# Second feed-forward of a two-layer backbone: products of 512 columns for the high weight halves, and feature sums spread out

## The chip, the cores and the metric

The kernel runs on one core of one Trainium2 chip, as one program and one launch. The metric is device time in microseconds. The kernel before took 2392.74 us, the median of 3 runs (2392.0 to 2393.63). One execution was also recorded by the hardware profiler, and every row quoted below is from that record.

The engines in the profile are PE (TensorE, the matmuls; PEld are its weight loads), DVE (VectorE), ACT (ScalarE), POOL (GpSimd) and SP, whose queue issues the transfers from memory.

## The reference, cut to what matters

Two trunk layers run over two groups of 128 tokens each (a prompt and a latent sample) with the same weights. Each layer is a mixer followed by a gated convolutional feed-forward, with an adaptive norm (shift, scale and gate computed from a condition vector) around both. The feed-forward is the part that the change touches:

```python
def conv_ffn(h, w_up, w_conv, b_conv, w_down):
    u = h @ w_up
    up = jnp.pad(u, ((0, 0), (1, 1), (0, 0)))
    u = up[:, :-2] * w_conv[0] + up[:, 1:-1] * w_conv[1] + up[:, 2:] * w_conv[2] + b_conv
    gate, val = u[..., :D_FF], u[..., D_FF:]
    return (jax.nn.silu(gate) * val) @ w_down

mod = jax.nn.silu(cond) @ w_ada[l] + b_ada[l]
sh1, sc1, gt1, sh2, sc2, gt2 = jnp.split(mod[:, None, :], 6, axis=-1)
x = x + gt2 * conv_ffn(h, w_ffn_up[l], w_ffn_conv[l], b_ffn_conv[l], w_ffn_down[l])
```

The model width is 2048, D_FF is 5632, and everything is float32.

## The kernel before

**Layout.** All activations lie with features on the 128 partitions and tokens along the free dimension. The two groups stand side by side, so an operand has NT = 256 columns.

**Split products.** A float32 product is made of three float32r products. Every operand x is kept as a high half (x rounded to float32r) and a low half (the rest), next to each other: `hx[:, k, :256]` and `hx[:, k, 256:512]`, and likewise the feed-forward's inner tiles `g`. Every 128 x 128 weight block is split in the same way into `wh` and `wl`, when it has been loaded: ACT casts the high half (L204), DVE subtracts to get the low half (L205), 8 blocks at a time. `gemm` (L278) then runs over the blocks of a product and issues wh x high (L285), wh x low (L286) and wl x high (L287), all three into the same 256 columns of a PSUM bank `acc`. There are three such banks, four buffers each for `wh` and `wl`, and three for the loaded tiles `raw` of 16 blocks.

**The feed-forward.** `ffn` (L919) runs in two rounds, each over half of the inner features. `up` (L941) makes 44 products of 16 blocks, alternately gate and value. After each, `conv` (L928) reads the bank three times: ACT (L930) and twice DVE (L933, L936). A pair is then multiplied and split into a `g` tile. `down` (L959) makes 16 products of 22 blocks over these g tiles, and `residual` (L512) adds each to x by two DVE operations (L515). In the last round the squares of x are summed on the way, for the final norm. The first three of the 88 up products of a layer are made by `first_three` (L255) while the norm before them is still running; they come to `ffn` in the list `ready`.

**Work in between.** The shifts, scales and gates come from a product with `w_ada`, 201 MB of weights for two columns. They are cut into units (layer, part, quarter) and made beside the rest of the kernel in two ways. Some units run on PE (`row_step`). Others are feature sums on DVE (`feature_step`, L355, recorded on L363): one pass of DVE over a 128 x 2048 tile for each of the two conditions, so that a loaded tile `araw` serves two sums and a unit takes eight. `pump` (L428) is called after each product and counts a rate up; when a whole step is due it issues one. In the up-projections the rate of feature sums is `FRATE["up"]`, 0.75 for each product. In the second feed-forward three units are left for the feature sums: 24 sums, the gate of its own residual. So after the first `up`, `ensure(l, 5)` issues all that are still missing, before the first `down`.

**Order.** The program is written in the order of the code. A scheduler then orders each engine's instructions by a simulated timeline, and on the chip each engine takes them strictly in that order. The feature sums keep the order of the code among themselves. Transfers are issued by SP in order, and each waits there until its buffer is free.

Of the kernel before, what the change touches and what calls it, by code (L numbers as in the profile page):

```python
# [13 lines left out]
ALU = mybir.AluOpType  # L14
# [3 lines left out]
P = 128  # L18
# [3 lines left out]
NT = 2 * T  # L22
# [26 lines left out]
    _n += _w  # L49
NCONST = _n  # L50
RATE = {"in": 0.4, "in3": 0.25, "heads": 0.85, "out0": 1.2, "c": 0.65, "outc": 0.65}
FRATE = {"up": 0.75, "down": 1.47}
PEW = {"heads": 1.0, "out0": 1.0, "c": 0.5}
QUIET = [4, 3, 3]

# [4 lines left out]
LATE = 3  # L60
# [21 lines left out]
def step_kernel(ctx: ExitStack, tc: tile.TileContext, A: dict):  # L82
    nc = tc.nc
    pe, dve, act, pool, sp = nc.tensor, nc.vector, nc.scalar, nc.gpsimd, nc.sync
# [3 lines left out]
    tmp = ctx.enter_context(tc.tile_pool(name="tmp", bufs=2))  # L88
    small = ctx.enter_context(tc.tile_pool(name="small", bufs=4))
    pacc = ctx.enter_context(tc.tile_pool(name="pacc", bufs=3, space=PSUM))  # L90
# [5 lines left out]
    def banks(name):  # L96
        return tc.tile_pool(name=name, bufs=1, space=PSUM)
# [3 lines left out]
    def nm(s):  # L101
        uid[0] += 1
        return f"{s}_{uid[0]}"

    def T_(pl, shape, tag, dt=F32, bufs=None):
        kw = {} if bufs is None else {"bufs": bufs}
        return pl.tile(shape, dt, tag=tag, name=nm(tag), **kw)
# [95 lines left out]
    def split(out_hi, out_lo, src):  # L203
        act.copy(out_hi, src)  # L204
        dve.tensor_tensor(out=out_lo, in0=src, in1=out_hi.bitcast(F32), op=ALU.subtract)  # L205
# [72 lines left out]
    def gemm(blocks, xh, xl, n=NT, first=0):  # L278

        ps = T_(pacc, [P, 512], "acc")  # L280
        last = len(blocks) - 1
        for i in range(last + 1):
            k = (i + first) % (last + 1)
            wh, wl = blocks[k]
            pe.matmul(ps[:, :n], wh, xh(k), start=(i == 0), stop=False)  # L285
            pe.matmul(ps[:, :n], wh, xl(k), start=False, stop=False)  # L286
            pe.matmul(ps[:, :n], wl, xh(k), start=False, stop=(i == last))  # L287
        return ps[:, :n]

# [57 lines left out]
    def load_row():  # L349
        feat["row"] = T_(feat["home"], [P, 2, D], "condb")  # L350
        sp.dma_start(out=feat["row"], in_=A["condb"])
        for r in range(2):
            act.activation(feat["row"][:, r], feat["row"][:, r], AF.Silu)

    def feature_step():  # L355

        l, j, q = FEATS[feat["i"]]
        t, c = divmod(feat["t"], 2)
        out = mod[:, l, j, 4 * q:4 * q + 4]
        if c == 0:  # L360
            feat["raw"] = T_(wpool, [P, 4, 512], "araw", bufs=2)
            sp.dma_start(out=feat["raw"], in_=A["w_ada"][l, j, q, t])
        tc.keep_in_program_order(dve.tensor_tensor_reduce(  # L363
            out=T_(feat["pool"], [P, D], "junk"), in1=feat["row"][:, c],
            in0=feat["raw"].rearrange("p g n -> p (g n)"), scale=1.0, scalar=0.0,
            op0=ALU.mult, op1=ALU.add, accum_out=out[:, t, c:c + 1]))
        feat["t"] += 1
        if feat["t"] == 8:
            dve.tensor_tensor(out=out, in0=out, in1=vector("bada", l, j, q), op=ALU.add)
            scales(l, j, q, out)  # L370
            feat["i"] += 1
            feat["t"] = 0
# [55 lines left out]
    def pump(rows, feats=0.0, until=None):  # L428

        until = until or RLIMIT[stage[0]]  # L430
        step()
        ada["due"] += rows
        while ada["due"] >= 0.25:
            if ada["i"] >= until and not later:
                ada["due"] = 0.0
                break
            dve_or_none = ada["i"] >= until or ada["i"] in SUMMED
            ada["due"] -= 0.25 if dve_or_none else 0.25 * ada["pew"]
            row_step(until)
        feat["due"] += feats  # L440
        while feat["due"] >= 1.0 and feat["i"] < FLIMIT[stage[0]]:
            feat["due"] -= 1.0
            feature_step()

    def ensure(l, j, qs=range(4)):
        for u in [(l, j, q) for q in qs]:
            while u in ROWS and ada["i"] <= ROWS.index(u):
                row_step()
            while u in FEATS and u not in done:
                feature_step()  # L450
            while u not in done:
                later.pop(0)()
# [59 lines left out]
    def residual(ps, l, which, c, st=None):  # L512
        for g in range(2):
            s = slice(g * T, (g + 1) * T)
            dve.scalar_tensor_tensor(out=x[:, c, s], in0=ps[:, s],  # L515
                                     scalar=mod[:, l, 3 * which + 2, c, g:g + 1],
                                     in1=x[:, c, s], op0=ALU.mult, op1=ALU.add)
        if st is not None:
            stat_add(st, x[:, c], KD)
# [398 lines left out]

    def ffn(hx, W, ready, l, st):  # L919
        xh, xl = (lambda k: hx[:, k, :NT]), (lambda k: hx[:, k, NT:2 * NT])  # L920
        product = lambda: ready.pop(0) if ready else gemm(W.chunk(), xh, xl)
        WD = Weights(A["w_down"][l], KQ, TB)
        cw = ada["cw"]
        with tc.tile_pool(name=f"ffn{l}", bufs=1) as fp, banks(f"pffn{l}") as pf:
            feat["home"], feat["pool"] = fp, pf
            T_(fp, [P, SHIFT // 4], "pad")

            def conv(ps, m):  # L928
                y = T_(fp, [P, NT], "cv", bufs=3)
                act.activation(y, ps, AF.Identity, scale=cw[:, 1, m:m + 1], bias=cw[:, 3, m:m + 1])  # L930
                y3 = y.rearrange("p (g t) -> p g t", g=2)
                p3 = ps.rearrange("p (g t) -> p g t", g=2)
                dve.scalar_tensor_tensor(out=y3[:, :, 1:], in0=p3[:, :, :T - 1],  # L933
                                         scalar=cw[:, 0, m:m + 1], in1=y3[:, :, 1:],
                                         op0=ALU.mult, op1=ALU.add)
                dve.scalar_tensor_tensor(out=y3[:, :, :T - 1], in0=p3[:, :, 1:],  # L936
                                         scalar=cw[:, 2, m:m + 1], in1=y3[:, :, :T - 1],
                                         op0=ALU.mult, op1=ALU.add)
                return y

            def up(q):  # L941
                gs = []
                for i in range(q * KQ, (q + 1) * KQ):
                    rate = 0 if i < LATE else FRATE["up"]
                    fine[0] = False
                    gate = conv(product(), i)
                    pump(0, rate)
                    if i == 0:
                        load_row()
                    val = conv(product(), NFF + i)  # L950
                    pump(0, rate)
                    act.activation(gate, gate, AF.Silu)
                    dve.tensor_tensor(out=val, in0=gate, in1=val, op=ALU.mult)
                    g = T_(fp, [P, ROW], "g", F32R, bufs=KQ)
                    split(g[:, :NT], g[:, NT:2 * NT], val)
                    gs.append(g)
                return gs

            def down(gs, q):  # L959
                for c in range(KD):  # L960
                    quiet = q == NQ - 1 and c >= KD - QUIET[0]
                    fine[0] = quiet
                    ps = gemm(WD.chunk(), lambda k: gs[k][:, :NT], lambda k: gs[k][:, NT:2 * NT])
                    residual(ps, l, 1, c, st if q == NQ - 1 else None)
                    pump(0, 0 if quiet else FRATE["down"])

            for q in range(NQ):
                gs = up(q)
                if q == 0:
                    ensure(l, 5)  # L970
                down(gs, q)
            while feat["i"] < FLIMIT[stage[0]]:
                feature_step()


    with banks("pab") as ppool["ada"]:
# [8 lines left out]
        hx = T_(keep, [P, KD, ROW], "hx", F32R)  # L985
# [3 lines left out]
        W = Weights(A["w_up"][0], KD, 1)  # L989
        hx, ready = modulated(st, 0, 1, W)  # L990
    stage[0] = "ffn0"
    st = stat_init()
    ffn(hx, W, ready, 0, st)
    stage[0] = "c"
    with tc.tile_pool(name="cc", bufs=1) as cp, banks("pc") as ppool["ada"]:
        ada["pool"] = cp
        ppool["att"] = ppool["ada"]
        W = Weights(A["w_in_c"], KD, 1)
        hx, ready = modulated(st, 1, 0, W)
# [4 lines left out]
        W = Weights(A["w_up"][1], KD, 1)  # L1004
        hx, ready = modulated(st, 1, 1, W)
    stage[0] = "ffn1"
    st = stat_init()
    ffn(hx, W, ready, 1, st)
    rb = norm_scale(st)
    for c in range(KD):  # L1010
# [131 lines left out]
```

## Time and profile before

| | |
|---|---|
| Median of 3 runs | 2392.74 us |
| The profiled execution | 2393.78 us |
| Its span, first to last instruction | 2391.9 us |
| Mean granted TensorE clock | 0.986 |
| Mean transfer rate from memory | 256 GB/s |
| First feed-forward, about | 505 to 1200 us |
| Second feed-forward, about | 1660 to 2377 us |
| Its first and second down-projection begin at | 1898.2 and 2257.2 us |

A row of the page's groups names the line, the engine, the operation, the tiles (written <- read), the shape and the count; then the busy time and the mean duration in ns, and the idle time of the engine ahead of these instructions with what ended it. Matmuls are pipelined: the recorded time of one runs into the next, and the distance between the starts of two tells what one costs. In the chain of waits each row is a start, a length and a piece of work, back from the last instruction.

### The profile page before, as it was taken

To read this page: it belongs to the slowest core of one execution; us is meant where nothing else is said; L and a number is where in the kernel's file an instruction comes from. 1 tells how busy PE (TensorE), PEld (TensorE's weight loads), DVE (VectorE), ACT (ScalarE), POOL (GpSimd) and SP (SyncE) were. 2 spreads that over 40 slices of the span, in tenths; PEclk is the share of its full clock that TensorE was granted. 3 is DMA by queue.
4 is the path that set the end of the run, shared out by engine and by line. 5 is a ranking of instruction groups with operands and counts; after the bars stand their busy time and mean duration, and the time that the engine had idled before them with its cause. 6 is when DMAs were issued, how large, how long until landed. Compare 5 with 4: busy or idle time off the path is not lost.

```text
span 2391.9 us, 47258 instructions
## 1 busy us (share of the span) xinstructions
PE 2321.7 (97%) x19628; PEld 2189.1 (92%) x19628; DVE 1782.0 (75%) x2714; ACT 1161.1 (49%) x1814; POOL 176.0 (7%) x211
## 2 busy tenths in 40 slices
PE   6999999999999999999989999998999999999997
PEld 3778868789999999999979999997999999999997
DVE  2457544479999999999977798886899755666654
ACT  4435545355554345554454454445555534555542
POOL 2002101110000000001210000122000000000011
PEclk8999999999999999999989999999999999999999
DMA  9886677877777877777857777776677555555553
GB/s 377 319 334 243 231 272 305 314 288 256 270 266 283 299 277 265 267 265 284 302 225 275 268 270 292 249 272 252 224 265 265 195 194 194 194 194 194 194 194 122
DMA packets 92551, 612.93 MB, mean 256 GB/s; under 512 B 9969, under 2 KB 17841, under 8 KB 20401
## 3 DMA queue, kind: packets, MB, share of 16 engines
q1 hardware_dynamic: 92336, 609.91, 69.5%
q8 instruction: 154, 2.52, 0.4%
q14 instruction: 61, 0.49, 0.1%
HBM read 605.12 MB, written 4.75 MB: 255 GB/s over the span
## 4 chain that ended last, share of the span: by engine, by line
PE 92%; DVE 3%; DMA 3%; issue 1%; ACT 1%; POOL 0%; SPq 0%; POOLq 0%; DVEq 0%; ACTq 0%
PE acc L285 27%; PE acc L286 27%; PE acc L287 27%; PE ada L378 4%; DMA araw<-w_ada 1%; PE acc L269 1%; DVE aacc L407 1%; PE acc L270 1%; DVE wl L205 1%; PE acc L271 1%; PE att L564 1%; DMA ckc<-cache_ckv 1%; DMA raw<-w_in_ab 0%; PE ada L326 0%; PE att L855 0%
## 5 line engine op out<-in xcount | busy, mean ns | idle before, releaser
L204 ACT CAST wh<-raw 128x1024 fp32r<-128x1024 f32 (+1 forms) x788 | 793.9, 1013 | 984.4 <-PE acc L286 868.8
L205 DVE TENSOR_TENSOR wl<-raw,wh 128x1024 fp32r<-128x1024 f32 (+1 forms) x788 | 923.5, 1184 | 388.6 <-ACT wh L204 383.9
L285 PE MATMUL acc<-hx,wh 128*128 128x256 f32 x4064 | 1132.3, 279 | 9.2 <-ACT hx L472 6.2
L286 PE MATMUL acc<-hx,wh 128*128 128x256 f32 x4064 | 1130.2, 278 | 0.0
L287 PE MATMUL acc<-hx,wl 128*128 128x256 f32 x4064 | 1129.9, 278 | 0.0
L285 PEld LDWEIGHTS acc<-hx,wh 128*128 128x128 f32 x4064 | 765.7, 189 | 36.6 <-issue 13.0
L286 PEld LDWEIGHTS acc<-hx,wh 128*128 128x128 f32 x4064 | 766.1, 189 | 15.3 <-issue 14.4
L287 PEld LDWEIGHTS acc<-hx,wl 128*128 128x128 f32 x4064 | 765.6, 188 | 9.3 <-issue 9.1
L286 PE MATMUL acc<-g,wh 128*128 128x256 f32 x1408 | 388.2, 276 | 0.0
L287 PE MATMUL acc<-g,wl 128*128 128x256 f32 x1408 | 388.1, 276 | 0.0
L285 PE MATMUL acc<-g,wh 128*128 128x256 f32 x1408 | 388.0, 276 | 0.0
L363 DVE CUSTOM_DVE_ANT_0 junk<-araw,condb 128x2048 f32<-128x2048 f32 x128 | 293.2, 2291 | 0.0
L286 PEld LDWEIGHTS acc<-g,wh 128*128 128x128 f32 x1408 | 264.2, 188 | 0.0
L287 PEld LDWEIGHTS acc<-g,wl 128*128 128x128 f32 x1408 | 264.2, 188 | 0.0
L285 PEld LDWEIGHTS acc<-g,wh 128*128 128x128 f32 x1408 | 264.1, 188 | 0.0
L170 POOL TENSOR_TENSOR sqacc<-sqacc,sq 128x256 f32<-128x256 f32 x76 | 93.8, 1234 | 1529.2 <-issue 1223.1
L378 PE MATMUL ada<-araw,condw 128*32 128x512 f32 x832 | 116.6, 637 | 27.7 <-DMA araw<-w_ada 22.7
L407 DVE SCALAR_TENSOR_TENSOR aacc<-araw,condw,aacc 128x512 f32<-128x512 f32 x150 | 112.4, 773 | 0.2
L930 ACT ACTIVATE cv<-acc,convw 128x256 f32<-128x256 f32 x176 | 98.1, 559 | 0.0
L515 DVE SCALAR_TENSOR_TENSOR x<-acc,mod,x 128x128 f32<-128x128 f32 x192 | 58.4, 344 | 45.3 <-PE acc L287 44.3
L936 DVE SCALAR_TENSOR_TENSOR cv<-acc,convw,cv 128x254 f32<-128x254 f32 x176 | 84.4, 480 | 3.8
L933 DVE SCALAR_TENSOR_TENSOR cv<-acc,convw,cv 128x254 f32<-128x254 f32 x176 | 83.7, 476 | 0.0
(207 smaller groups left out, 1812.9 us busy)
## 6 DMA issues: line engine op xcount, KB each, us to landing
araw<-w_ada SPq DMA_DIRECT2D x188, 1024.0 KB, 5.6
raw<-w_up SPq DMA_DIRECT2D x176, 1024.0 KB, 4.8
raw<-w_down SPq DMA_DIRECT2D x88, 1024.0 KB, 4.8
raw<-w_in_c SPq DMA_DIRECT2D x48, 1024.0 KB, 5.5
raw<-w_in_ab SPq DMA_DIRECT2D x20, 1024.0 KB, 7.2
raw<-w_out_ab SPq DMA_DIRECT2D x16, 1024.0 KB, 6.9
raw<-w_out_c SPq DMA_DIRECT2D x16, 1024.0 KB, 4.8
raw<-w_q_up SPq DMA_DIRECT2D x6, 768.0 KB, 4.7
```

The costliest lines, as they stand in the source:

```text
L170: pool.tensor_tensor(out=st["acc"], in0=st["acc"], in1=sq, op=ALU.add)
L204: act.copy(out_hi, src)
L205: dve.tensor_tensor(out=out_lo, in0=src, in1=out_hi.bitcast(F32), op=ALU.subtract)
L285: pe.matmul(ps[:, :n], wh, xh(k), start=(i == 0), stop=False)
L286: pe.matmul(ps[:, :n], wh, xl(k), start=False, stop=False)
L287: pe.matmul(ps[:, :n], wl, xh(k), start=False, stop=(i == last))
L363: tc.keep_in_program_order(dve.tensor_tensor_reduce(out=T_(feat["pool"], [P, D], "junk"), in1=feat["row"][:, c], in0=feat["raw"].rearrange ...
L378: i = pe.matmul(ada["ps"][32 * g:32 * g + 32, :], condw[:, 4 * t + g, :], raw[:, g], start=(t == 0), stop=(t == 3), skip_group_check=True)
L407: i = dve.scalar_tensor_tensor(out=acc[:, c], in0=raw[:, g], scalar=condw[:, k, c:c + 1], in1=acc[:, c], op0=ALU.mult, op1=ALU.add)
L930: act.activation(y, ps, AF.Identity, scale=cw[:, 1, m:m + 1], bias=cw[:, 3, m:m + 1])
L933: dve.scalar_tensor_tensor(out=y3[:, :, 1:], in0=p3[:, :, :T - 1], scalar=cw[:, 0, m:m + 1], in1=y3[:, :, 1:], op0=ALU.mult, op1=ALU.add)
L936: dve.scalar_tensor_tensor(out=y3[:, :, :T - 1], in0=p3[:, :, 1:], scalar=cw[:, 2, m:m + 1], in1=y3[:, :, :T - 1], op0=ALU.mult, op1=ALU.add)
```

## The change

In the second feed-forward (layer index 1) `gemm` is replaced by `gemm_wide`. The high weights meet both halves of the operand in one matmul of 512 columns, which writes the whole bank: wh x high into the first 256 columns, wh x low into the others. The matmul of the low weights adds wl x high to the second 256. In the last block the low weights come first. The two halves of the bank are summed on the way out: ACT copies the second half to a tile `nt`, DVE adds the first half to it, and `conv` and `residual` read this tile in place of the bank. The three products of `first_three` stay as they were, and so does the first feed-forward.

The rate of the feature sums in the up-projection becomes one for each layer: 0.75 in the first, as before, and 0.35 in the second.

```diff
-FRATE = {"up": 0.75, "down": 1.47}
+FRATE = {"up": (0.75, 0.35), "down": 1.47}
...
+    def gemm_wide(blocks, x2):
+        ps = T_(pacc, [P, 512], "acc")
+        last = len(blocks) - 1
+        for i, (wh, wl) in enumerate(blocks):
+            if i < last:
+                pe.matmul(ps, wh, x2(i), start=(i == 0), stop=False)
+            pe.matmul(ps[:, NT:], wl, x2(i)[:, :NT], start=False, stop=False)
+        pe.matmul(ps, wh, x2(last), start=False, stop=True)
+        u = T_(tmp, [P, NT], "nt", bufs=4)
+        act.copy(u, ps[:, NT:])
+        dve.tensor_tensor(out=u, in0=ps[:, :NT], in1=u, op=ALU.add)
+        return u
...
-        product = lambda: ready.pop(0) if ready else gemm(W.chunk(), xh, xl)
+        wide = l == 1
+
+        def product():
+            if ready:
+                return ready.pop(0)
+            return gemm_wide(W.chunk(), lambda k: hx[:, k]) if wide else gemm(W.chunk(), xh, xl)
...
-                    rate = 0 if i < LATE else FRATE["up"]
+                    rate = 0 if i < LATE else FRATE["up"][l]
...
-                    ps = gemm(WD.chunk(), lambda k: gs[k][:, :NT], lambda k: gs[k][:, NT:2 * NT])
+                    if wide:
+                        ps = gemm_wide(WD.chunk(), lambda k: gs[k])
+                    else:
+                        ps = gemm(WD.chunk(), lambda k: gs[k][:, :NT], lambda k: gs[k][:, NT:2 * NT])
```

The built programs show what this moves. In the rows below a number behind a name tells one buffer from the next.

PE, the first two blocks of the first down-projection's first product, before:

```order
L285 MATMUL acc_22356<-g_19566,wh_22338 128x256
L286 MATMUL acc_22356<-g_19566,wh_22338 128x256
L287 MATMUL acc_22356<-g_19566,wl_22339 128x256
L285 MATMUL acc_22356<-g_19638,wh_22338 128x256
L286 MATMUL acc_22356<-g_19638,wh_22338 128x256
L287 MATMUL acc_22356<-g_19638,wl_22339 128x256
```

and the first three blocks of it now:

```order
L297 MATMUL acc_21823<-g_19566,wh_21805 128x512
L298 MATMUL acc_21823<-g_19566,wl_21806 128x256
L297 MATMUL acc_21823<-g_19625,wh_21805 128x512
L298 MATMUL acc_21823<-g_19625,wl_21806 128x256
L297 MATMUL acc_21823<-g_19730,wh_21805 128x512
L298 MATMUL acc_21823<-g_19730,wl_21806 128x256
```

A block is two matmuls where it was three; each has one weight load of its own.

DVE, where the first down-projection begins (`g` is the last g tile's low half, `wl` are low halves of weights, `junk` are feature sums), before:

```order
L205 TENSOR_TENSOR g_22333<-cv_22327,g_22333 128x256
L205 TENSOR_TENSOR wl_22432<-raw_22425,wh_22431 128x1024
L515 SCALAR_TENSOR_TENSOR x_76<-acc_22356,mod_77,x_76 128x128 x2
L205 TENSOR_TENSOR wl_22507<-raw_22504,wh_22506 128x1024
L205 TENSOR_TENSOR wl_22511<-raw_22504,wh_22510 128x1024
L205 TENSOR_TENSOR wl_22517<-raw_22514,wh_22516 128x1024
L515 SCALAR_TENSOR_TENSOR x_76<-acc_22435,mod_77,x_76 128x128 x2
```

and now:

```order
L205 TENSOR_TENSOR g_21766<-cv_21760,g_21766 128x256
L378 ISA junk_21769,mod_77<-araw_21655,condb_19556 128x2048
L378 ISA mod_77 128x1
L378 ISA junk_21773,mod_77<-araw_21771,condb_19556 128x2048
L378 ISA mod_77 128x1
L205 TENSOR_TENSOR wl_21936<-raw_21933,wh_21935 128x1024
L302 TENSOR_TENSOR nt_21868<-acc_21823,nt_21868 128x256
L378 ISA junk_21775,mod_77<-araw_21771,condb_19556 128x2048
L378 ISA mod_77 128x1
L205 TENSOR_TENSOR wl_21940<-raw_21933,wh_21939 128x1024
L530 SCALAR_TENSOR_TENSOR x_76<-nt_21868,mod_77,x_76 128x128 x2
L205 TENSOR_TENSOR wl_21946<-raw_21943,wh_21945 128x1024
```

All 24 feature sums of this stage stood ahead of this place before. Now 13 do, and 11 stand behind it, among the first eight down products. The sum of the bank's two halves (L302) stands ahead of each residual (L530).

PE, where that first down product (acc_22356 before, acc_21823 now) reads the last g tile in its last block, before:

```order
L285 MATMUL acc_22356<-g_22333,wh_22348 128x256
L285 MATMUL acc_22435<-g_19566,wh_22348 128x256
L286 MATMUL acc_22435<-g_19566,wh_22348 128x256
L287 MATMUL acc_22435<-g_19566,wl_22349 128x256
L285 MATMUL acc_22435<-g_19638,wh_22348 128x256
L286 MATMUL acc_22356<-g_22333,wh_22348 128x256
L287 MATMUL acc_22356<-g_22333,wl_22349 128x256
```

and now, behind seventeen matmuls of the next product, acc_21883:

```order
L297 MATMUL acc_21883<-g_20372,wh_21819 128x512
L298 MATMUL acc_21823<-g_21766,wl_21816 128x256
L298 MATMUL acc_21883<-g_20372,wl_21820 128x256
L297 MATMUL acc_21883<-g_20481,wh_21819 128x512
L298 MATMUL acc_21883<-g_20481,wl_21820 128x256
L297 MATMUL acc_21883<-g_20588,wh_21875 128x512
L298 MATMUL acc_21883<-g_20588,wl_21876 128x256
L297 MATMUL acc_21883<-g_20693,wh_21875 128x512
L298 MATMUL acc_21883<-g_20693,wl_21876 128x256
L299 MATMUL acc_21823<-g_21766,wh_21815 128x512
```

Four matmuls of the next product stood ahead of this tile's low half before, and none ahead of its high half; now 24 and 17 do.

## The prediction

> **What bounds the kernel now.** I read the page's busy shares and the chain that ended last first, to find the engine that sets the end.
>
> ```profile
> PE 2321.7 (97%) x19628; PEld 2189.1 (92%) x19628; DVE 1782.0 (75%) x2714; ACT 1161.1 (49%) x1814; POOL 176.0 (7%) x211
> PE 92%; DVE 3%; DMA 3%; issue 1%; ACT 1%; POOL 0%; SPq 0%; POOLq 0%; DVEq 0%; ACTq 0%
> ```
>
> TensorE (PE) is busy for 97% of the span and holds 92% of the chain. Then the table by stretches, for the stage that the change touches. Its columns are length of the stretch, then busy us of PE, weight loads (PEld), DVE, ACT and POOL with their counts, granted clock, DMA share and GB/s.
>
> ```profile
> 1690.00:2377.00 687.00, 687.00 (x6065) 687.00 (x6063) 474.95 (x623) 334.78 (x441) 16.41 (x14) 1.00 0.57 204
> 1700.00:1800.00 100.00, 100.00 (x885) 100.00 (x884) 94.40 (x120) 53.10 (x73) 0.00 (x0) 1.00 0.72 265
> 1898.00:1950.00 52.00, 52.00 (x462) 52.00 (x461) 28.23 (x35) 20.89 (x22) 0.00 (x0) 1.00 0.55 192
> 2377.00:2392.00 15.00, 2.21 (x11) 1.34 (x9) 7.61 (x21) 0.42 (x1) 0.70 (x1) 0.61 0.34 140
> ```
>
> From 1690 to 2377 us PE never stops and the clock is fully granted. DVE comes close in the first up-projection (94.4 of 100 us), and has much to spare in the first down-projection (28.2 of 52). Last, who waits for whom from 1690 to 2370 us:
>
> ```profile
> ACT wh L204 <- PE acc L286: 298.1, 215, 1.7
> DVE wl L205 <- ACT wh L204: 184.9, 166, 1.5
> ```
>
> PE waits for nobody: no row names it as the one that waits. The others wait for PE to free a weight buffer. So only two things count: how long PE takes for the matmuls of this stage, and whether something makes it wait that does not now.
>
> **The matmuls.** Per block of weights PE now does three float32r products of 256 columns, each with its own weight load. From 1600 us on:
>
> ```profile
> L285 PE MATMUL acc<-hx,wh 128*128 128x256 f32 x1360 | 376.2, 277 | 2.1 <-DVE mod L337 2.1
> L285 PE MATMUL acc<-g,wh 128*128 128x256 f32 x704 | 194.0, 276 | 0.0
> ```
>
> 1360 + 704 = 2064 blocks go through the function that is replaced. A recorded duration is that of a pipelined matmul, so the price is the distance between starts. The chain of waits gives it:
>
> ```profile
> 2330.15 0.11 PE acc L285
> ...
> 2344.43 0.11 PE acc L285
> ```
>
> 42 blocks lie between these two starts, and 14.28 / 42 = 340.0 ns a block, 113.3 a matmul. After the change a block is one product of 512 columns and one of 256. The 256 I leave at 113.3, since its successor's weight load still has to run beside it, as here, where the load for L286 starts with the matmul of L285:
>
> ```profile
> 1690.79 0.28 PE L285 MATMUL acc<-hx,wh 128*128 128x256 f32 x1
> 1690.79 0.19 PEld L286 LDWEIGHTS acc<-hx,wh 128*128 128x128 f32 x1
> ```
>
> The question is the 512, of which this trace has no float32r example. But the first layer's heads run the same three-product function at 384 columns:
>
> ```profile
> 329.49 0.34 PE L285 MATMUL acc<-kv_in,wh 128*128 128x384 f32 x1
> ...
> 330.01 0.34 PE L285 MATMUL acc<-kv_in,wh 128*128 128x384 f32 x1
> ...
> 330.53 0.34 PE L285 MATMUL acc<-kv_in,wh 128*128 128x384 f32 x1
> ```
>
> Three matmuls lie between neighbouring rows, so 0.52 / 3 = 173.3 ns each. 128 more columns cost 60.0 ns, **more** than half of 113.3 (56.7). Had a matmul a fixed cost of its own, that wide ones save, 128 columns would cost less than half. Going on along the line, 512 columns take 113.3 + 2 x 60.0 = 233.3 ns, and a block 233.3 + 113.3 = 346.7: 6.7 ns more than now.
>
> The bound from below comes from plain float32 matmuls, whose records each are one pass:
>
> ```profile
> L855 PE MATMUL att<-dk,dq 128*128 128x256 f32 x32 | 9.6, 380 | 0.0
> L855 PE MATMUL att<-dk,dq 128*128 128x128 f32 x32 | 6.1, 273 | 0.0
> ```
>
> There 128 columns cost 107 ns. If float32r streams at twice that pace at best, 128 columns cost 53.5, and 512 take 113.3 + 107 = 220.3: 6.4 ns a block less than now. I take 233.3, since the 384-column row is the same function, type and engine state; the plain pass is another mode. **Term: 2064 x 6.7 ns = +13.8 us**, with -13.1 as its other end.
>
> The Trainium skill (TensorE: Matmul & The Clock Gate, Back-to-back issue gap) has a warm matmul cost N / 2.4 + 2.5 ns: 109.2, 162.5 and 215.8 for 256, 384 and 512 columns. The trace has 113.3 and 173.3 for the first two, 4 and 11 ns above, with a miss that grows with the width. By that rule the new block takes 325 ns and the sum becomes about -29 us; it is written for bf16, and I give it a small chance below.
>
> **Leaving PSUM.** Each of the 117 wide products (85 up, 32 down) gets an ACT copy and a DVE add:
>
> ```profile
> L830 ACT COPY dev<-acc 128x256 f32<-128x256 f32 x32 | 11.7, 366 | 1.1 <-DVE dq L532 1.1
> L709 DVE TENSOR_TENSOR proj<-proj,acc 128x256 f32<-128x256 f32 x45 | 18.6, 418 | 23.0 <-PE acc L287 22.7
> ```
>
> ACT gets 43 us more in 687 (335 now), DVE 49 (475 now). All but the last lie beside PE's next product; three accumulator banks give two products, over 10 us, to empty one. Both wait for a product's last matmul; behind them stand the next high half on ACT and the next low half on DVE, which PE needs only three halves (8 us) later, so a wait of a microsecond there reaches nobody. The last stands on the path:
>
> ```profile
> 2377.11 0.61 DVE L515 SCALAR_TENSOR_TENSOR x<-acc,mod,x 128x128 f32<-128x128 f32 x2 [6.87 <-PE acc L287]
> 2377.81 0.42 ACT L166 ACTIVATE sq<-x 128x256 f32<-128x256 f32 x1 [7.06 <-DVE x L515]
> ```
>
> From DVE's end (2377.72) to ACT's start is 0.09 us. The copy, one such step and the add: 0.37 + 0.09 + 0.42 = **+0.9 us** of tail. The reads that move from PSUM to SBUF I cost at nothing, under PE's cover.
>
> **The feature sums.** 24 of them run in this stage:
>
> ```profile
> L205 DVE TENSOR_TENSOR wl<-raw,wh 128x1024 fp32r<-128x1024 f32 x240 | 292.6, 1224 | 177.4 <-ACT wh L204 174.1
> L363 DVE CUSTOM_DVE_ANT_0 junk<-araw,condb 128x2048 f32<-128x2048 f32 x24 | 55.0, 2290 | 0.0
> L363 DVE DVE_READ_ACCUMULATOR2_ANT mod<- 128x1 f32 x24 | 3.4, 141 | 0.0
> L515 DVE SCALAR_TENSOR_TENSOR x<-acc,mod,x 128x128 f32<-128x128 f32 x60 | 18.2, 345 | 12.9 <-PE acc L287 12.9
> ```
>
> Each takes 2.29 + 0.14 = 2.43 us. In the first up-projection a pair of products loses 0.8 of them (1.5 to 0.7) and gains two adds: -1.94 + 0.84 = -1.1 us in 10.9, so DVE falls from 94% to some 84%. But at 0.35 only 13 are done there. The other 11 are forced behind it, where the built order spreads them over the first down-projection. Between the sums of its first and eighth product DVE has 18 low halves, 9 feature sums, 7 adds and 7 pairs of residual updates: 22.0 + 21.9 + 2.9 + 4.8 = 51.7 us, beside 7 x 22 blocks = 154 x 0.3467 = 53.4 us of PE. That is 97% where it was 54%. Three halves (8 us) of split weights stand ahead of PE when it begins. Bounds: nothing, if this lead holds; 6 us, if DVE's in-order waits for sums eat a tenth of the stretch. I take **+1 us**. The five loads that move with them wait on SP for DVE to free a tile, ahead of weight loads; those have 5.5 us a tile and land sooner:
>
> ```profile
> raw<-w_down SPq DMA_DIRECT2D x88, 1024.0 KB, 4.8
> ```
>
> **From up to down.** The first down product needs the last g in its last block. In the built order ACT makes two more weight halves before it, the second of which waits for block 15: 16 x 0.347 + 1.05 (cast) + 1.22 (low half) + 0.42 = 8.2 us, with 1.05 from here:
>
> ```profile
> L204 ACT CAST wh<-raw 128x1024 fp32r<-128x1024 f32 x258 | 271.9, 1055 | 348.9 <-PE acc L286 305.4 <-issue 36.7 <-PE acc L270 4.9
> ```
>
> PE comes to it only after 21 + 8.5 blocks, 10.2 us, since 17 matmuls of the next product were put ahead. Cost nothing; without that cover about 1 us, twice.
>
> **Sum.** The profiled execution took 2393.78 us (span 2391.9), 1.04 above the median 2392.74. 13.8 + 0.9 + 1 = +15.7 gives 2409.5 for it, **2408.4** against the median.
>
> **Rivals** (all but the first term kept, +1.9).
> - *A fixed cost per matmul* (the other side): 384 columns are odd, and 512 keep only the excess that 256 have. Then 220.3, a block 333.7, 2064 x -6.4 = -13.1, and 2381.5. For it: one matmul and one load fewer. Against it: the 384 row. It decides from 226.7 ns down, twice 113.3. Chance 0.21.
> - *A cost per 256 columns begun*: 256 pays it once, 384 and 512 twice, so 512 takes 226.7, a block 340.0; the change does nothing on PE. 2394.6. It fits both rows as well as the line. Chance 0.18.
> - *Nothing but columns*: 6 x 53.5 = 321 ns a block, if all excess hangs on weight loads that the wide product now hides. -39 us, 2355. Nothing in the 384 row, whose loads are hidden too, supports it. Chance 0.09. The page's 325 belongs here.
> - *The slow rhythm*: matmuls of the mixer stage sometimes lock at a larger distance.
>
> ```profile
> 1301.95 0.28 PE L285 MATMUL acc<-hx,wh 128*128 128x256 f32 x1
> ...
> 1302.31 0.28 PE L285 MATMUL acc<-hx,wh 128*128 128x256 f32 x1
> ...
> 1302.66 0.28 PE L285 MATMUL acc<-hx,wh 128*128 128x256 f32 x1
> ```
>
> 0.355 us a block, 5 ns more per matmul. The alternating stream might lock there: two matmuls, 10 ns, +20.6 us on top, 2429. Chance 0.06.
>
> **How the numbers follow.** The line has 0.46, by itself 2403 to 2414 (its 0.9, and 0 to 6 for DVE). Faster: 0.21 + 0.09 = 0.30; within 0.2% (4.8 us, about what a measurement of this kernel can tell from no change): 0.18; slower: 0.46 + 0.06 = 0.52. The range runs from 2379 to 2414: it takes in the line, the 256-column granule and the fixed cost, and leaves out 0.15.
>
> **What would show it.** The distance between starts of the L297 and L298 rows decides: 233 and 113 by the line, 227 by the granule, 220 by a fixed cost. DVE near 97% with PE still 100% between 1900 and 1960 us shows the feature sums hidden; a wait of PE for wl there shows them not. The last sum must stand 0.9 us behind the last matmul. I am wrong if 512 columns take less than twice 256.

## The result, and the profile after

| | before | after |
|---|---|---|
| Median | 2392.5 us (4 runs, 2392.0 to 2393.63) | 2424.01 us (4 runs, 2418.81 to 2426.59) |
| Profiled execution (span) | 2393.78 (2391.9) | 2426.59 (2424.7) |
| Mean granted TensorE clock in it | 0.986 | 0.984 |

The changed kernel is **slower**: ratio 1.0128, 95% interval 1.0113 to 1.0143, +31.5 us between the medians. The direction was the likeliest one of the forecast; the time lies outside its range (2379 to 2414), and the loss is twice the +15.7 forecast. In some executions below, kernels whose feed-forwards are both narrow took 26 us more than in their others; the two groups are given apart, and e_rates_only shows where that time goes.

The page of after, busy times and the chain that ended last by engine:

```profile
PE 2353.7 (97%) x17564; PEld 2125.6 (88%) x17564; DVE 1827.1 (75%) x2831; ACT 1200.1 (49%) x1931; POOL 176.2 (7%) x211
PE 92%; DVE 3%; DMA 3%; issue 1%; ACT 1%; POOL 0%; SPq 0%; POOLq 0%; DVEq 0%; ACTq 0%
```

2064 matmuls fewer, and PE is busy for 32 us more. The chain is as before: 92% PE. Now the table by stretches of after (columns as in the prediction: length, then PE, PEld, DVE, ACT, POOL, clock, DMA share, GB/s):

```profile
1750.00:1890.00 140.00, 140.00 (x796) 121.71 (x795) 117.39 (x168) 80.62 (x126) 0.00 (x0) 1.00 0.63 216
1900.00:1960.00 60.00, 60.00 (x343) 52.21 (x342) 55.60 (x71) 27.36 (x36) 0.00 (x0) 1.00 0.72 259
```

PE is still full at full clock, also from 1900 to 1960 us, where DVE makes the feature sums that were put off (93% busy). Nothing new makes PE wait; its matmuls themselves got dearer. Two or three counted matmuls had begun ahead of each stretch: 794 in 140 us are 397 blocks, 353 ns each. The timeline of after has the distances:

```profile
1800.12 0.40 PE L297 MATMUL acc<-hx,wh 128*128 128x512 f32 x1
1800.36 0.28 PE L298 MATMUL acc<-hx,wl 128*128 128x256 f32 x1
1800.47 0.40 PE L297 MATMUL acc<-hx,wh 128*128 128x512 f32 x1
1800.71 0.28 PE L298 MATMUL acc<-hx,wl 128*128 128x256 f32 x1
1800.83 0.40 PE L297 MATMUL acc<-hx,wh 128*128 128x512 f32 x1
```

0.71 us for two blocks. Over all starts of the stage L297 takes 234.5 ns and **L298 takes 118.5**, where the forecast had 233.3 and 113.3. A block is 352.9 ns instead of 340.0. First and last matmul of the stage, in the timeline of before and then of after:

```profile
1673.45 0.36 PE L285 MATMUL acc<-hx,wh 128*128 128x256 f32 x1 [2.07 <-DVE mod L337]
...
2376.79 0.28 PE L287 MATMUL acc<-g,wl 128*128 128x256 f32 x1
```

```profile
1678.91 0.47 PE L297 MATMUL acc<-hx,wh 128*128 128x512 f32 x1 [2.06 <-DVE mod L352]
...
2408.69 0.39 PE L299 MATMUL acc<-g,wh 128*128 128x512 f32 x1
...
2409.12 0.37 ACT L301 COPY nt<-acc 128x256 f32<-128x256 f32 x1 [5.77 <-PE acc L299]
2409.53 0.42 DVE L302 TENSOR_TENSOR nt<-acc,nt 128x256 f32<-128x256 f32 x1 [6.69 <-ACT nt L301]
2409.99 0.61 DVE L530 SCALAR_TENSOR_TENSOR x<-nt,mod,x 128x128 f32<-128x128 f32 x2
```

The profiled executions differ by 32.8 us of span. The matmuls of the stage went from 703.3 to 729.8 us: **+26.4**. From the last start to the end of the span it was 15.1 and is 16.0 us: **+0.9**, the copy and the add. The other 5.5 lie ahead of the stage's first matmul, where both traces have the same instructions in the same order on every engine. So they are no work that the change added, and they vary: e_first_half below, with the same instructions there too, came to the stage 3.6 us sooner than after. The traces of e_split, e_grouped, e_pairs, e_one_wide and e_all512 have the same matmuls in the same order up to there, and all eight reach the stage between 1669.5 and 1678.9 us.

### The profile page after: what moved, and what is told of

Read it like the earlier page. It is cut to its first block, busy times and chain, and to the rows that moved or that the text cites. A ratio compares the mean times of both kernels' runs of the same rounds, so it can differ in the third digit from the quotient of the medians.

```text
span 2424.7 us, 43151 instructions
## 1 busy us (share of the span) xinstructions
PE 2353.7 (97%) x17564; PEld 2125.6 (88%) x17564; DVE 1827.1 (75%) x2831; ACT 1200.1 (49%) x1931; POOL 176.2 (7%) x211
## 4 chain that ended last, share of the span: by engine, by line
PE 92%; DMA 3%; DVE 3%; issue 1%; ACT 1%; POOL 0%; SPq 0%; POOLq 0%; DVEq 0%; ACTq 0%
PE acc L297 19%; PE acc L285 17%; PE acc L286 17%; PE acc L287 17%; PE acc L298 10%; PE ada L393 4%; DMA araw<-w_ada 2%; PE acc L299 1%; PE acc L269 1%; PE acc L270 1%; DVE aacc L422 1%; PE acc L271 1%; DVE wl L205 1%; PE att L579 1%; DMA ckc<-cache_ckv 1%
## 5 line engine op out<-in xcount | busy, mean ns | idle before, releaser
L285 PE MATMUL acc<-hx,wh 128*128 128x256 f32 x2704 | 757.2, 281 | 6.3 <-ACT hx L487 5.6
L286 PE MATMUL acc<-hx,wh 128*128 128x256 f32 x2704 | 755.1, 280 | 0.0
L285 PEld LDWEIGHTS acc<-hx,wh 128*128 128x128 f32 x2704 | 510.6, 189 | 33.2 <-issue 11.3
L286 PEld LDWEIGHTS acc<-hx,wh 128*128 128x128 f32 x2704 | 511.1, 189 | 15.7 <-issue 15.0
L297 PE MATMUL acc<-hx,wh 128*128 128x512 f32 x1275 | 455.4, 398 | 2.1 <-DVE mod L352 2.1
L298 PE MATMUL acc<-hx,wl 128*128 128x256 f32 x1360 | 369.1, 282 | 0.0
L297 PEld LDWEIGHTS acc<-hx,wh 128*128 128x128 f32 x1275 | 240.3, 188 | 57.5 <-ACT wh L204 2.3
L298 PEld LDWEIGHTS acc<-hx,wl 128*128 128x128 f32 x1360 | 255.9, 188 | 7.7
L297 PE MATMUL acc<-g,wh 128*128 128x512 f32 x672 | 237.9, 397 | 0.0
L286 PE MATMUL acc<-g,wh 128*128 128x256 f32 x704 | 194.0, 276 | 0.0
L285 PE MATMUL acc<-g,wh 128*128 128x256 f32 x704 | 194.0, 276 | 0.0
L298 PE MATMUL acc<-g,wl 128*128 128x256 f32 x704 | 192.6, 281 | 0.0
L297 PEld LDWEIGHTS acc<-g,wh 128*128 128x128 f32 x672 | 125.8, 188 | 29.4
L298 PEld LDWEIGHTS acc<-g,wl 128*128 128x128 f32 x704 | 132.1, 188 | 2.9
```

The lines of the kernel that those rows point to most:

```text
L297: pe.matmul(ps, wh, x2(i), start=(i == 0), stop=False)
L298: pe.matmul(ps[:, NT:], wl, x2(i)[:, :NT], start=False, stop=False)
```

## The experiments

In all of them a block time is the mean distance between neighbouring starts of the stage in the trace, times three matmuls (narrow) or summed over two (wide). Letters such as A or B name the theories of the expectation above a result. Lines of an edit that are left out are marked by dots.

**e_split.** The wide product in two halves; all else of the change stays.

```diff
-                pe.matmul(ps, wh, x2(i), start=(i == 0), stop=False)
+                pe.matmul(ps[:, :NT], wh, x2(i)[:, :NT], start=(i == 0), stop=False)
+                pe.matmul(ps[:, NT:], wh, x2(i)[:, NT:2 * NT], start=False, stop=False)
...
```

> Kernel: after, with each 512-column product issued as two products of 256 columns into the two halves of the same bank; bank layout, copy, add and feature-sum rates stay as in after. Theory A (the price lies in the width: the 512 itself and the 256 that follows it): all matmuls return to 113.3 ns, a block to 340.0 ns, and the time to about 2394 to 2395 us (before, plus 0.9 us of tail). Rival B (the price lies in what comes with the wide form: the second half of the bank, the copy and the add, the other rates): the matmuls stay near 118 ns, a block near 353 ns, about 2419 to 2424 us. Rival C (a cost of the feature-sum burst or of the exit path that no matmul spacing shows, some 5 us of the 31): spacing 113.3 but 2398 to 2400 us.

Measured: six executions at 2392.0 to 2395.0, four at 2418.9 to 2421.2; before beside it, twelve at 2390.2 to 2397.8 and seven at 2417.0 to 2421.6. The stretch of e_split that answers to the one above:

```profile
1750.00:1890.00 140.00, 140.00 (x1238) 140.00 (x1237) 120.88 (x174) 82.99 (x129) 0.00 (x0) 1.00 0.64 229
```

Some 1236 matmuls in 140 us: 113.3 ns, a block 340.0 again. Copy, add, bank layout and feature sums together cost no more than the tail. The loss hangs on the width (A); B and C fall.

**e_first_half.** `pe.matmul(ps[:, :NT], wl, ...)` in place of `ps[:, NT:]`.

> Kernel: after, with the low-weight product added to the first half of the bank instead of the second (the halves are summed on the way out, so the result is the same sum). Theory A (a 256 behind a 512 costs 118.5 ns because of the widths): nothing changes, 2419 to 2427 us, L298 at 118.5 ns. Rival D (the 256 waits for columns of the bank that the 512 has just written): L298 falls to 113.3 ns, or the next 512 pays instead, since it then begins in the half just written: about 2413 us in the first case, same time with the 5 ns moved to L297 in the second.

Measured: 2425.6 us (2420.5 to 2428.4), 234.5 and 118.5 ns, as in after. Which half of the bank is written doesn't matter; D falls.

**e_grouped and e_pairs.** Two other orders of the same products: eight 512s and then eight 256s; and every second block with its two products exchanged, of which the core is:

```diff
-            if i < last:
+            if i % 2 == 0 and i < last:
                 pe.matmul(ps, wh, x2(i), start=(i == 0), stop=False)
             pe.matmul(ps[:, NT:], wl, x2(i)[:, :NT], start=False, stop=False)
...
+            if i % 2 == 1 and i < last:
+                pe.matmul(ps, wh, x2(i), start=False, stop=False)
...
```

> Kernel: after, with the products of each 8 blocks reordered: eight of 512 columns, then eight of 256, so that only one 256 in eight follows a 512. Theory A1 (118.5 ns belongs to a 256 directly behind a 512, and the 512 costs the line's 233.3 by itself): mean block 233.3 to 234 plus 113.3 to 114, about 347.5 ns, 2064 x 5.4 = 11 us less than after, about 2411 us. Rival A2 (after the first 512 the whole stream is in a slower rhythm, whatever the order): 256s stay at 117 to 118.5 ns, block 353 ns, 2419 to 2424 us.

> Kernel: after, with the two products of every second block exchanged, so that the widths run 512, 256, 256, 512, 512, 256: half as many changes of width. Theory A1 (each change of width from 512 to 256 costs its 6 ns over 346.7, and equal neighbours cost nothing): block about 350 ns, 2418 us or less. Rival A2 (any 512 in the stream keeps it in the slower rhythm): 353 ns, as after, 2419 to 2427 us. Rival A3 (equal neighbours let it settle at once): 346.7 ns, 2411 us.

Measured: e_grouped 2413.4 us (2410.0 to 2419.4) with 349.2 ns a block in the up-projections and 347.8 in the down-projections; e_pairs **2408.7** us (2404.9 to 2412.4) with 346.7 and 347.0. The timeline of e_pairs (L300 is the exchanged 512; x2 are two 256s):

```profile
1800.34 0.40 PE L297 MATMUL acc<-hx,wh 128*128 128x512 f32 x1
1800.58 0.39 PE L298 MATMUL acc<-hx,wl 128*128 128x256 f32 x2
1800.81 0.39 PE L300 MATMUL acc<-hx,wh 128*128 128x512 f32 x1
1801.03 0.40 PE L297 MATMUL acc<-hx,wh 128*128 128x512 f32 x1
```

0.69 us for two blocks: the same matmuls in another order, and 346.7 ns, the very block that the forecast had. But not by the prices expected. The distances are 235.8 for a 512 before a 256, 118.3 for a 256 before a 256, 113.3 for a 256 before a 512 and 225.8 for a 512 before a 512. A matmul has no price of its own here; its price depends on its neighbours. A2 falls. A1 comes near for e_grouped and A3 has the block of e_pairs, both with the wrong reason, since equal neighbours are not free: in e_grouped whole groups of 256s stand at 118, others fall to 113 behind their first two. The exchange also changes the order in which the weight tiles are used; no run separates that from the order of the widths.

**e_all512.** `pe.matmul(ps, wl, x2(i))`: low x low is added too, so that only 512s are left.

> Kernel: after, with the low-weight product widened to 512 columns as well (it adds low x low, which after leaves out), so that the stage is one stream of 512-column products, 4128 of them. If 512 columns cost the line's 233.3 ns by themselves: 466.7 ns a block, distance 233.3; if the slow excess is on every 512: 235 ns, 470. If there is a saving from an unbroken wide stream: below 230 ns. Time about 2424 + 2064 x 0.115 = 2661 us.

Measured: 2661.0 us, 466.7 ns a block. Its timeline:

```profile
1799.85 0.39 PE L297 MATMUL acc<-hx,wh 128*128 128x512 f32 x1
1800.08 0.40 PE L298 MATMUL acc<-hx,wl 128*128 128x512 f32 x1
1800.32 0.39 PE L297 MATMUL acc<-hx,wh 128*128 128x512 f32 x1
...
1801.25 0.39 PE L297 MATMUL acc<-hx,wh 128*128 128x512 f32 x1
```

Six 512s in 1.40 us: 233.3 each on the mean (230.8 and 235.5 in turn). In this stream the line through 256 and 384 holds to 512.

**e_rates_only and e_one_wide.** Before with the new rates alone; before with a single wide product in the stage.

```diff
-FRATE = {"up": 0.75, "down": 1.47}
+FRATE = {"up": (0.75, 0.35), "down": 1.47}
...
```

> Kernel: before, with the change's feature-sum rates alone (0.35 in the second up-projection, 11 sums forced into the first down-projection), products narrow. Theory A (all of the loss is matmul time): as before, 2390 to 2394 us. Rival C (the sums cost something): 2395 us or more with waits of PE for wl behind the up-projection. Aside: some executions of before and of the split kernel on this chip took 2417 to 2421 us instead of 2390 to 2395; if the profiled one is of that kind, theory R (the whole last stage has then fallen into the slower rhythm) expects 117.7 ns instead of 113.3 between starts there, 6192 x 4.4 = 27 us; a rival (an outside disturbance) expects 113.3 and the loss elsewhere.

> Kernel: before, with one product of the last stage in the wide form (the first after the three that are made ahead), all others narrow, rates as before. Theory R1 (the slower rhythm, once entered behind a 512, stays until something breaks it): all executions near 2418 to 2421 us and 117.7 ns through the stage. Rival R2 (the stream of 256s falls back on its own after a few matmuls): 2390 to 2395 us as often as before, 113.3 ns behind the wide product.

Measured: e_rates_only took 2389.8 to 2392.3 us in five executions and 2418.7 to 2423.9 in five; e_one_wide 2392.6 (2389.9 to 2394.5) in all ten, with 113.3 ns behind its wide product. The rates cost nothing (C falls), and a 512 doesn't leave the stream behind it in a slower rhythm (R1 falls). The profiled execution of e_rates_only was a long one. The first layer's feed-forward in it, and then in e_one_wide:

```profile
600.00:1100.00 500.00, 500.00 (x4248) 500.00 (x4247) 452.93 (x568) 236.32 (x309) 0.00 (x0) 1.00 0.72 264
```

```profile
600.00:1100.00 500.00, 500.00 (x4414) 500.00 (x4413) 469.31 (x589) 248.57 (x322) 0.00 (x0) 1.00 0.74 273
```

At the same full clock and with PE always busy, 117.8 ns a matmul against 113.3; the second layer's stage stood at 113.3 in the same execution. The expectation R had the size right and the layer wrong. The whole first feed-forward, the same code, stands in a slower rhythm: 2064 x 13.3 ns = 27.5 us. One trace shows this; that the other long executions are of the same kind is inferred from their times.

**Where the weights lie.** In before and after the weight tiles begin 64 bytes behind `hx` and `g`, counted modulo 256 (`hx` and `g` at byte 96 of 512, the weight tiles at byte 160). A row of `hx` or `g` has 2048 bytes and a weight block 512, so all blocks of a stage have one distance. Two pads, unused columns of four bytes, set it, and the next runs change them:

```diff
-    T_(wpool, [P, 48], "pad", bufs=1)
+    T_(wpool, [P, 64], "pad", bufs=1)
...
-            T_(fp, [P, SHIFT // 4], "pad")
+            T_(fp, [P, SHIFT // 4 - 32], "pad")
```

These are the edits of e_dist_128_192, made in the kernel after. e_dist_32_96 has 40 and SHIFT // 4 - 8, e_dist_160_224 has 72 and SHIFT // 4 - 40; e_weights_96 and e_weights_352 have 32 and 96 in the first and leave the second.

> Kernel: after, with the 192-byte pad ahead of the weight tiles cut to 128 bytes, so that the weights begin at byte 96 of 512 instead of 160, as hx does; the g tiles move along to 32, so that their distance to the weights stays. Theory S (the 118.5 ns and the excess of the 512 come from how operand and weights lie to each other in SBUF): the up-projections change from 353 ns a block, the down-projections don't. Theory T (they come from the absolute place of the operand): the down-projections change, the up-projections don't. Theory A (they come from the alternation of widths alone): 353 ns in both, 2419 to 2427 us.

> Kernel: after, with the pad at 384 bytes, so that the weights begin at byte 352 of 512 (256 behind hx's 96) and g at 288. Theory S: up-projections change, down-projections (same distance as in after) don't. Theory T: down changes, up doesn't. Theory A: 353 ns in both, 2419 to 2427 us. Best case for either, 346.7 ns a block: 2411 us.

> Kernel: after, with the weight tiles 128 bytes (mod 256) behind hx and 192 behind g; in before and after it is 64 for both, and e_weights_96 and e_weights_352 had 0 for hx. The narrow products of the first layer's feed-forward and the wide ones of the second lie alike, so one run shows four distances. At 64 narrow matmuls took 113.3 ns (block 340) and wide blocks 353; at 0 they took 120.0 (block 360) and 354.3. Theory S (weight load and operand read meet in SBUF, and the distance decides how often): narrow distances other than 113.3, and a wide block that moves by a few ns; if some distance frees both, narrow 106.7 to 110 ns and wide 320 to 340. Theory W (the wide form pays its own 353 to 354, wherever the weights lie): wide blocks 352 to 355 at 128 and at 192, whatever the narrow ones do. Time 2419 to 2475 us by what the narrow ones do.

> Kernel: after, with the weight tiles 32 bytes behind hx and 96 behind g (mod 256). Same theories: S expects narrow between the 113.3 of 64 and the 120.0 of 0 at 32, and a wide block that differs from 353; W expects the wide block at 352 to 355 in both.

> Kernel: after, with the weight tiles 160 bytes (mod 256) behind hx and 224 behind g. So far the wide block took 353.0 ns at distance 64, 353 to 354 at 0, 354.1 at 32, 347.1 at 96, 352 at 128 and at 192, and the narrow block 340.0 at 64 and 353 to 360 at all others. Theory W (no layout brings the wide form, with widths in turn, to the 340 of the narrow form at 64): wide 346 to 355 at both, narrow 350 to 360. Rival V (some distance suits the wide form as 64 suits the narrow one): a wide block below 340 at 160 or at 224.

Measured: 2468.2, 2469.8, 2465.8, 2463.1 and 2469.4 us (the last from one execution). The narrow products of the first layer and of the mixers move too, so these times say little of the wide form. The blocks do; each run shows the narrow one in the first layer's feed-forward and the wide one in the second's:

| Distance (mod 256) | 0 | 32 | 64 | 96 | 128 | 160 | 192 | 224 |
|---|---|---|---|---|---|---|---|---|
| Narrow block, ns | 360.0 | 355.0 | **340.0** | 352.0, 356.0 | 356.0 | 360.0 | 353.3 | 350.0 |
| Wide block, ns | 353.3 | 353.1 | 352.9 | 347.1 | 350.9 | 350.4 | 351.7 | 347.6 |

0, 32, 128 and 160 are from hx, 96, 192 and 224 from g. 64 is from both: e_weights_96 and e_weights_352 moved g along with the weights and kept 340.1 and 353.0 there, so the distance counts and not the place. That 256 counts as 0 is shown by one pair: hx stands 0 bytes ahead of the weights in e_weights_96 and 256 in e_weights_352, with 360.0 in both. **The narrow block is cheap at one of the eight distances tried, the one that the kernel has; the wide block never costs below 347.** S and T both missed what matters: it is the narrow form that depends on the layout. A had the wide block right in the first two runs, and the time wrong. W missed its first range, 352 to 355, at 96, 128 and 192; its later one, 346 to 355, holds. V falls.

Distance isn't all. At 96 the first down-projection took 352.0 and the second 356.0, in one trace; at 224 a later trace of the same program (e_wide_160_224) took 353.3 where this one took 350.0. And before itself has two rhythms at 64, in two stretches of the second mixer, with the same `hx` and the same weight tiles:

```profile
1304.00:1317.00 13.00, 13.00 (x112) 13.00 (x112) 12.49 (x23) 8.11 (x17) 0.65 (x1) 1.00 0.78 263
1424.00:1439.00 15.00, 15.00 (x135) 15.00 (x134) 14.49 (x28) 8.65 (x17) 0.00 (x0) 1.00 0.68 254
```

By their starts that is 353.3 and 340.0 ns a block. Each stretch is an unbroken stream, and such a stream keeps its rhythm to its end; between the two stand other matmuls, of the attention and of `w_ada`. The first feed-forward is one unbroken stream from 511 to 1234 us in e_rates_only, all of it at 353.3. What settles the rhythm at a stream's start is open.

**e_pairs_96.** The order of e_pairs with 96 as the distance to both.

> Kernel: the exchanged order (512, 256, 256, 512) at distance 96 of the weight tiles from hx and from g. The exchanged order took 346.7 ns a block at 64, and the alternating one 347.1 at 96. If the two gains add: 341 ns or less. If they are the same stalls, seen from two sides: 346 to 348 ns. Narrow products of the first layer at 96, for hx and g: about 353 ns a block, if distance 64 is the only good place for them.

Measured: 352.6 and 352.1 ns a block, narrow 356.0, 2463.7 us. Both theories miss: the better order and the better distance don't add, and together they are worse than either.

**e_narrow_160_224 and e_wide_160_224.** Before and after in one and the same other layout, the pads being 72 and SHIFT // 4 - 40.

> Kernel: before (narrow products in both layers), with the weight tiles 160 bytes behind hx and 224 behind g, as e_dist_160_224 has them. Theory L (the sign of the change is set by the layout: the narrow form is cheap only at distance 64): the last stage takes its first layer's 360 and 350 ns a block, 1360 x 360 + 704 x 350 = 736.0 us, against 1360 x 350.7 + 704 x 347.6 = 721.7 us of the wide form there; so 14.3 us, less 0.9 of tail, 13.4 us more than the wide kernel in the same layout, about 2482.8 us. Rival W (the wide form is dearer by itself): 13 to 31 us less than the wide kernel in that layout, 2438 to 2456 us.

> Kernel: e_dist_160_224 once more (the changed kernel in that layout), beside the narrow one on the same chip: about 2469.4 us by theory L and by W.

Measured: narrow 2480.9 us (2477.3 to 2481.9), wide **2471.2** (2470.6 to 2474.1). The change makes this kernel 9.7 us faster, and the two ranges don't touch. L holds (2482.8 and 2469.4 expected), and W, with 2438 to 2456 for the narrow one, falls. The same stretch of the narrow one and then of the wide one:

```profile
1750.00:1890.00 140.00, 140.00 (x1169) 140.00 (x1169) 125.70 (x162) 70.07 (x98) 0.00 (x0) 1.00 0.68 249
```

```profile
1750.00:1890.00 140.00, 140.00 (x801) 122.09 (x800) 116.70 (x167) 81.43 (x126) 0.00 (x0) 1.00 0.64 218
```

Three matmuls of 120.0 ns, 360 a block, against 140 us over some 399 blocks, 351. From first to last start the stage took 735.9 us narrow and 722.8 wide, where theory L had 736.0 and 721.7; of those 13.1 less 0.9 of tail the medians show 9.7. The sign of the change depends on the layout. No version tried beats before in its own layout; the wide one here is still some 79 us behind it.

## Why the prediction was right and wrong

- **What bounds the kernel: right.** PE is full at full clock in the stage, before and after.
- **The 512 at 233.3: right here.** 233.3 in a pure stream, 234.5 in turn with 256s. The fixed cost (220.3), the granule (226.7) and the rival of nothing but columns fall for these streams; in the order of e_pairs a 512 takes 225.8 or 235.8 by what follows it.
- **"The 256 I leave at 113.3": this is the step that failed.** It took the price of a 256 from a stream of 256s, and gave as reason that its successor's weight load runs beside it as before. In turn with a 512 it costs 118.5. With the 1.1 ns more of the 512 that is 6.3 ns a block, 2064 x 6.3 = 13 us of the miss. e_split shows that it takes the mixed widths (340.0 without them), and e_pairs that the order counts: the same matmuls take 346.7 there. That its 2408.7 us meets the forecast of 2408.4 is luck: of its four distances only the 113.3 of a 256 before a 512 is one that the forecast used.
- **The slow rhythm: the rival that came.** It had 355 ns a block in the mixer stage as its evidence and the alternating stream as its place, and got 0.06. It put the 5 ns on both matmuls and on top of the line (2429); they came nearly all on the 256. Whether the mixer's rhythm and this one have one cause is not shown. The range left it out. The prediction saw in the trace that the same matmul stands at 113.3 and at 118 in one kernel, and still treated 113.3 as the price of 256 columns.
- **The tail, +0.9: right**, 15.1 to 16.0 us.
- **Feature sums +1 (0 to 6), transition 0, cover of copy and add: right in kind.** DVE stood at 93% where 97% was worked out, PE at 100%; e_rates_only costs nothing.
- **Where the rest lies.** 26.4 + 0.9 = 27.3 us of the 31.5 between the medians are in the stage and its tail. The other 4 are not located in the medians; the profiled executions differ by 5.5 ahead of the stage, where both kernels do the same work, and what makes that was not found. The miss of 15.6 us is so made of 12.6 for the matmuls (26.4 for 13.8), these 4, and 1 less for the feature sums.

## What to carry to other kernels

The price of a matmul, read from a stream, is that of this stream: of its widths, its order, where weights and operand lie in SBUF (the memory on the chip that TensorE reads them from), and the rhythm it fell into at its start. Before a stream is changed, look in the trace for the same instruction at two distances under a full clock; if there are two, give the dearer one a real share of the chance. A form that loses in one layout can win in another (-9.7 us here, +31.5 there), so move the operands a few dozen bytes before judging it.

## What the runs showed of the hardware

- Distances between float32r matmuls depend on the distance in SBUF between weights and operand, here counted modulo 256 bytes: 340 to 360 ns for three of 256 columns, with the clock at 1.00 and PE never idle.
- At one distance an unbroken stream of 256s can stand in more than one rhythm: 340.0 or 353.3 ns a block at 64 (before), 352.0 or 356.0 at 96 (e_dist_32_96).
- Four of the block times lie a whole number of 6.67 ns apart: 340.0, 346.7, 353.3, 360.0. Others don't (350.0, 355.0, 356.0, 352.9), and no run here shows a stall of a fixed length. The Trainium skill (TensorE: Matmul & The Clock Gate, Back-to-back issue gap) has N / 2.4 + 2.5 ns for an isolated warm matmul; an estimate from its first part is 320 ns for the 768 columns of a block; the least here is 340.0. The sustained 131 ns that the Trainium skill gives in the same section for N=512 are not what the traces here have for float32r: 233.3.
- The first feed-forward of narrow kernels at distance 64 takes 113.3 or 117.8 ns a matmul for its whole length, from one execution to the next (the traces of before and e_rates_only). Of 63 executions of before 19 took 2416.6 to 2423.8 us, the others 2389.7 to 2398.0. Of the 38 of after, e_first_half, e_grouped, e_pairs and e_one_wide none shows a jump of that size, though their first layers have the same instructions. Why is open. The comparison at the top had only the shorter kind of before; against a long one the changed kernel's 2424 us are some 5 us more.
